# Stick-breaking sums from high and low parts in float32r, with one more stage in their pipeline

## The chip, the core and the metric

The kernel runs on one core of a Trainium2 chip. The metric is the device time of one execution in microseconds (us); three executions of the kernel before gave 1900.29, 1902.61 and 1904.76 us, and the median, 1902.61 us, is the time that the prediction is compared with. TensorE (PE) does the matrix products, VectorE (DVE), ScalarE (ACT) and GpSimd (POOL) the elementwise work, and SyncE (SP) issues the transfers. Each engine works through its own queue in order.

## The reference, cut to what matters

Two layers of a decoder trunk act on a sequence of 256 tokens with 1024 channels. A layer projects its input once, runs four mixers on the result (block-sparse attention, retention, a state-space mixer called SSD, and stick-breaking attention), projects and merges them, and then applies a feed-forward part: dense in the first layer, two of eight experts in the second. The change is in the stick-breaking attention, of 8 heads of width 64:

```python
z = jnp.einsum('bqhd,bkhd->bhqk', qb, k).astype(jnp.float32) * scale
causal = kpos[None, :] < qpos[:, None]
log_beta = jax.nn.log_sigmoid(z)
log_1mb = jnp.where(causal, jax.nn.log_sigmoid(-z), 0.0)
rem = lax.cumsum(log_1mb, axis=3, reverse=True) - log_1mb
w = jnp.where(causal, jnp.exp(log_beta + rem), 0.0).astype(v.dtype)
return jnp.einsum('bhqk,bkhd->bqhd', w, v)
```

For each query the logarithms `log_1mb` are summed over all later keys (the reversed cumulative sum), and the exponentials of score plus sum are the weights of the values. The kernel works with L = softplus(z) = -log_1mb, whose sum including the key itself is taken away from z. So the sums are products of L with a matrix of zeros and minus ones, and they are added in PSUM to the scores that already stand there.

## The kernel before, in words

**The stream of weights.** All weights come from HBM as tiles of 128x2048 numbers (`raw`, 1 MB each). SP issues one transfer for each tile, in an order fixed when the program is built. A tile is used in two halves of 128x1024. For each half ACT copies it to float32r (`whi`, L310), and DVE subtracts that copy from the original (`wlo`, L317). PE then forms each product as three float32r matmuls, high by high, high by low and low by high (`mm3`, L417 to L419). A half is 24 such matmuls of 256 columns, or 12 of 512. Five halves can be held in split form, and `half` (L351) lets the split run up to three halves ahead of the one that PE multiplies (AHEAD = 3).

**The side work.** After the matmuls of each half, `half` calls `step()` once, at some places twice, and one step of a list of tasks is written into the program there. The tasks are generators: the mixers (`ssd_task`, `sb_task`, `moba_task`, `ret_task`), and a few smaller ones. The schedule is manual: an instruction stands in its engine's queue where the code issued it. So what stands between two parts of a task is the work of the halves: on ACT the copies `whi` and the evacuations of finished PSUM banks (L724, L710 and others), on DVE the subtractions `wlo` and the weighted sums of adaLN tiles (L473, two for each tile), on PE the 24 or 12 matmuls.

**Stick-breaking.** `sb_task` (L924) handles the 8 heads as four pairs, with the helper `pipeline` (L745): each pair goes through seven stages, a new pair begins every third step, and within a step the later stages are issued first. The stages before are: `scores` (PE, into two PSUM banks), `soft` (two DVE operations for each head at L949 and L950, then an exponential and a logarithm on ACT at L953 and L954), `plus` (POOL: an addition at L958, and `strict`, L932, which zeroes the entries that are not strictly causal), `sums` (PE, three float32 matmuls for each head, L963 to L965), `weights` (for each head DVE clips the diagonal blocks at L971, ACT takes the exponential at L973, POOL applies `strict`), `out_` (`values`, PE, L739 and L742), and `end` (`split` of the result into float32r parts: ACT L426 and DVE L427). With a step of three, one step issues `end`, `sums` and `scores` of three successive pairs, the next `weights` and `soft`, the third `out_` and `plus`. The pool `px` gives this side work four PSUM banks of 512 numbers in each partition (two pairs' scores), and `w3` gives six tiles of 128x384.

The constant NT (128x128, zeros and minus ones) and NEGO (a column of minus ones, read 128 times) are slices of the tile `cst`, in float32.

## Time and profile before

| | us |
|---|---|
| median of three executions | 1902.61 |
| the profiled execution's own time | 1908.61 |
| its span, first to last instruction | 1906.6 |
| PE busy | 1862.5 (98%) |
| DVE busy | 1592.1 (84%) |
| ACT busy | 1194.6 (63%) |
| POOL busy | 186.6 (10%) |

The profiled execution took 6.0 us more than the median, and 2.0 us of it lie outside its span. The mean granted TensorE clock was 0.992 of full speed. A row of a timeline gives the start in us from the start of the span, the busy time, the engine and the line of the code; "xN" says that N instructions of one kind stand in one row. Matmuls overlap in their pipeline, so their cost is read from the distance between the starts of two rows, not from the busy time. A number in brackets at the end of a row is the time that the engine sat idle just before it, with what released it.

### The profile page before, as it was taken

To read this page: it belongs to the slowest core of one execution; us is meant where nothing else is said; L and a number is where in the kernel's file an instruction comes from. 1 tells how busy PE (TensorE), PEld (TensorE's weight loads), DVE (VectorE), ACT (ScalarE), POOL (GpSimd) and SP (SyncE) were. 2 spreads that over 40 slices of the span, in tenths; PEclk is the share of its full clock that TensorE was granted. 3 is DMA by queue.
4 is the path that set the end of the run, shared out by engine and by line. 5 is a ranking of instruction groups with operands and counts; after the bars stand their busy time and mean duration, and the time that the engine had idled before them with its cause. 6 is when DMAs were issued, how large, how long until landed. Compare 5 with 4: busy or idle time off the path is not lost.

```text
span 1906.6 us, 28966 instructions
## 1 busy us (share of the span) xinstructions
PE 1862.5 (98%) x11162; PEld 1627.6 (85%) x11162; DVE 1592.1 (84%) x2009; ACT 1194.6 (63%) x1507; POOL 186.6 (10%) x205
## 2 busy tenths in 40 slices
PE   6999999999999999999999999999999999999997
PEld 5888999899989889999888888888888888888885
DVE  7777877787766787768899989989899899999997
ACT  4545634454446356444677777777777777777774
POOL 0023332000000123320000000000000000000000
PEclk9999999999999999999899999999999999999999
DMA  9565666587745465656899999999999999999992
GB/s 354 185 242 210 228 234 220 185 282 285 286 168 208 164 250 201 243 177 242 330 383 331 350 369 372 393 373 352 366 375 388 379 343 376 355 403 375 388 401 110
DMA packets 86804, 565.99 MB, mean 297 GB/s; under 512 B 10241, under 2 KB 10497, under 8 KB 24706
## 3 DMA queue, kind: packets, MB, share of 16 engines
q1 hardware_dynamic: 82226, 550.30, 76.7%
q0 software_dynamic: 4288, 13.65, 2.2%
q8 instruction: 89, 1.46, 0.3%
q14 instruction: 57, 0.47, 0.1%
q10 hardware_dynamic: 144, 0.11, 0.0%
HBM read 557.21 MB, written 6.82 MB: 296 GB/s over the span
## 4 chain that ended last, share of the span: by engine, by line
PE 92%; DVE 3%; DMA 2%; issue 1%; ACT 1%; POOL 0%; SPq 0%; DVEq 0%; ACTq 0%; POOLq 0%
PE mm L417 23%; PE mm L419 22%; PE mm L418 22%; PE mx L419 6%; PE mx L418 6%; PE mx L417 6%; PE mx L1540 1%; DMA raw<-in_win_dram 1%; PE mx L1407 1%; DMA raw<-in_adaT_dram 1%; PE mx L739 1%; DVE wlo L317 1%; DVE raw L473 0%; PE mx L963 0%; DVE a L781 0%
## 5 line engine op out<-in xcount | busy, mean ns | idle before, releaser
L317 DVE TENSOR_TENSOR wlo<-raw,whi 128x1024 fp32r<-128x1024 f32 (+1 forms) x878 | 1036.4, 1223 | 188.8 <-ACT whi L310 187.1
L310 ACT ACTIVATE whi<-raw 128x1024 fp32r<-128x1024 f32 (+1 forms) x880 | 879.6, 1050 | 127.2 <-DMA raw<-in_win_dram 23.8
L417 PE MATMUL mm<-whi,ghi 128*128 128x512 f32 x896 | 350.3, 391 | 0.0
L419 PE MATMUL mm<-whi,glo 128*128 128x512 f32 x896 | 349.1, 390 | 0.0
L418 PE MATMUL mm<-wlo,ghi 128*128 128x512 f32 x896 | 348.7, 389 | 0.0
L417 PE MATMUL mm<-hhi,whi 128*128 128x256 f32 x1024 | 293.1, 286 | 14.0 <-ACT whi L310 14.0
L419 PE MATMUL mm<-hhi,wlo 128*128 128x256 f32 x1024 | 286.4, 280 | 0.9 <-DVE wlo L317 0.9
L418 PE MATMUL mm<-hlo,whi 128*128 128x256 f32 x1024 | 286.3, 280 | 0.0
L417 PEld LDWEIGHTS mm<-hhi,whi 128*128 128x128 f32 x1024 | 194.4, 190 | 22.6 <-ACT whi L310 16.4
L419 PEld LDWEIGHTS mm<-whi,glo 128*128 128x128 f32 x896 | 168.2, 188 | 35.8
L418 PEld LDWEIGHTS mm<-wlo,ghi 128*128 128x128 f32 x896 | 168.2, 188 | 34.9 <-DVE wlo L317 0.2
L417 PEld LDWEIGHTS mm<-whi,ghi 128*128 128x128 f32 x896 | 168.2, 188 | 34.2
L419 PEld LDWEIGHTS mm<-hhi,wlo 128*128 128x128 f32 x1024 | 194.5, 190 | 1.4 <-DVE wlo L317 1.4
L418 PEld LDWEIGHTS mm<-hlo,whi 128*128 128x128 f32 x1024 | 194.5, 190 | 0.7 <-issue 0.5
L417 PE MATMUL mx<-whi,ehi 128*128 128x512 f32 x448 | 179.6, 401 | 0.0
L419 PE MATMUL mx<-whi,elo 128*128 128x512 f32 x448 | 175.1, 391 | 0.0
L418 PE MATMUL mx<-wlo,ehi 128*128 128x512 f32 x448 | 174.9, 390 | 0.0
L426 ACT ACTIVATE ehi<-mx 128x512 fp32r<-128x512 f32 x56 | 33.6, 600 | 112.9 <-PE mx L1540 112.9
L419 PEld LDWEIGHTS mx<-whi,elo 128*128 128x128 f32 x448 | 84.1, 188 | 18.0
L418 PEld LDWEIGHTS mx<-wlo,ehi 128*128 128x128 f32 x448 | 84.3, 188 | 16.4 <-DVE wlo L317 0.8
L417 PEld LDWEIGHTS mx<-whi,ehi 128*128 128x128 f32 x448 | 84.2, 188 | 15.7
L1500 POOL DMA_INDIRECT outs<-lnt,row x14 | 14.4, 1026 | 807.0 <-DVE lnt L1494 804.8
(382 smaller groups left out, 2921.5 us busy)
## 6 DMA issues: line engine op xcount, KB each, us to landing
raw<-in_egu_dram SPq DMA_DIRECT2D x205, 1024.0 KB, 7.4
raw<-in_edn_dram SPq DMA_DIRECT2D x96, 1024.0 KB, 7.3
raw<-in_win_dram SPq DMA_DIRECT2D x79, 1024.0 KB, 4.9
raw<-in_adaT_dram SPq DMA_DIRECT2D x31, 1024.0 KB, 5.4
raw<-in_fgu_dram SPq DMA_DIRECT2D x22, 1024.0 KB, 5.6
raw<-in_adaR_dram SPq DMA_DIRECT2D x16, 1024.0 KB, 4.9
raw<-in_wbr_dram SPq DMA_DIRECT2D x16, 1024.0 KB, 4.9
raw<-in_fdn_dram SPq DMA_DIRECT2D x11, 1024.0 KB, 5.0
```

The lines of the kernel that those rows point to most:

```text
L310: act.activation(hi[:, c], raw, AF.Copy)
L317: dve.tensor_sub(lo[:, c], raw, hi[:, c].bitcast(F32))
L417: pe.matmul(ps, a[0], b[0], start=start, stop=False, **kw)
L418: pe.matmul(ps, a[0], b[1], start=False, stop=False, **kw)
L419: pe.matmul(ps, a[1], b[0], start=False, stop=stop, **kw)
L426: act.activation(hi, src, AF.Copy)
L739: pe.matmul(o[64 * j:64 * j + 64, :], v[:, 0, 128 * p + 64 * j:128 * p + 64 * j + 64], ws[j][:, 0:256], start=True, stop=False, skip_group ...
L1407: pe.matmul(o, xs[t][part][:, k * P:(k + 1) * P], dsp[:, t].rearrange("p a b -> p (a b)"), start=(n == 0), stop=(n == 3))
L1500: nc.gpsimd.indirect_dma_start(outs[c][:, :], bass.IndirectOffsetOnAxis(ap=row[:, 0:1], axis=0), y, None)
L1540: pe.transpose(pt[:, k * P:(k + 1) * P], g[:, k * P:(k + 1) * P], ident)
```

## The change

The tile L of each head is split like a weight, into a float32r copy on ACT and the remainder on DVE, in a new stage `parts_` between `plus` and `sums`; each head takes two more tiles of `w3` for it. `sums` multiplies both parts with NT and NEGO, which are now float32r: six matmuls of one pass for each head in place of three float32 matmuls, each of which the trace shows as two instructions. The number of stages stays at seven, because the former `end` (the split of the result) now stands in the same stage as `values`. The constants move into a tile of their own, `negs`, filled once by a transfer from POOL and a copy on ACT in the SSD task of the first layer.

```diff
--- before.py
+++ after.py
@@ -42,8 +42,8 @@
     _i += 2 * _c
 NWIN = _i
 
-C_ID, C_M3, C_NT, C_AL, C_IO, C_NEG, C_DEC, C_END = np.cumsum(
-    [0, 128, 384, 128, 384, 257, 1, 1536]).tolist()
+C_ID, C_M3, C_AL, C_IO, C_NEG, C_NT, C_DEC, C_END = np.cumsum(
+    [0, 128, 384, 384, 257, 1, 128, 1536]).tolist()
 S_C, S_CW, S_CB, S_DS, S_NG, S_GG, S_GB, S_L1G, S_L1B, S_L2G, S_L2B, S_DTB, S_AL, S_SDT, S_BA, S_END = np.cumsum(
     [0, 8, 32, 8, 4, 4, 4, 4, 8, 8, 8, 8, 8, 8, 64, 48]).tolist()
 
@@ -433,7 +433,9 @@
     crow = rowp.tile([P, D], F32, name="crow", bufs=1)
     nc.sync.dma_start(crow[0:1, :], I["c"])
     nc.scalar.dma_start(sm[0], I["sm"][0])
-    cst = cp.tile([P, C_DEC], F32, name="cst")
+    cst = cp.tile([P, C_NEG], F32, name="cst")
+
+    negs = cp.tile([P, 129], F32R, name="negs")
     rt = cp.tile([P, 72], F32, name="rt")
     x = [xp.tile([P, D], F32, name=f"x{t}") for t in range(2)]
     xT = I["xT"].rearrange("p k t -> p (k t)")
@@ -446,8 +448,7 @@
     mask3 = cst[:, C_M3:C_M3 + 384]
     U = cst[:, C_M3:C_M3 + 128]
     ONE = one.to_broadcast([P, P])
-    NT = cst[:, C_NT:C_NT + 128]
-    NEGO = cst[:, C_NEG:C_NEG + 1].to_broadcast([P, P])
+    NEGO, NT = negs[:, 0:1].to_broadcast([P, P]), negs[:, 1:129]
     ALI = cst[:, C_AL:C_AL + 384]
     iota = cst[:, C_IO:C_IO + 257]
 
@@ -677,8 +678,8 @@
         def a4(dt=F32):
             return mp.tile([P, 1024], dt, name="a4", bufs=9)
 
-        def w3():
-            return mp.tile([P, 384], F32, name="w3", bufs=6)
+        def w3(dt=F32):
+            return mp.tile([P, 384], dt, name="w3", bufs=6)
 
         def part_T(pss, kh, k1, rhs, evac=None):
 
@@ -790,6 +791,9 @@
             yield from need("xbc")
             xs_, bcm = T["xca"]
             two = mp.tile([40, 256], F32R, name="two", bufs=1)
+            if l == 0:
+                raw = w3()[:, 0:129]
+                nc.gpsimd.dma_start(raw, I["cst"][:, C_NEG:C_DEC])
             act.activation(pick, ident[0:40, 0:8], AF.Copy)
             act.activation(pick[32:40], ident[32:40, 32:40], AF.Copy)
             pool.memset(two.bitcast(F32), 0.0)
@@ -815,6 +819,8 @@
             act.activation(ee, ee, AF.Exp)
             ea = mp.tile([P, 8], F32, name="ea", bufs=1)
             act.activation(ea, s[:, S_AL:S_AL + 8], AF.Exp)
+            if l == 0:
+                act.activation(negs, raw, AF.Copy)
             yield
 
             cbt = []
@@ -958,11 +964,18 @@
                     pool.tensor_tensor(L, L, m, op=ALU.add)
                     strict(L)
 
+            def parts_(p):
+                for j, (m, L) in enumerate(LL[p]):
+                    LL[p][j] = hi, lo = w3(F32R), w3(F32R)
+                    split(hi, lo, L)
+
             def sums(p):
-                for z, (m, L) in zip(zz[p], LL.pop(p)):
-                    pe.matmul(z[:, 0:256], NT, L[:, 0:256], start=False, stop=True, skip_group_check=True)
-                    pe.matmul(z[:, 128:256], NEGO, L[:, 256:384], start=False, stop=True, skip_group_check=True)
-                    pe.matmul(z[:, 256:384], NT, L[:, 256:384], start=False, stop=True, skip_group_check=True)
+                for z, hl in zip(zz[p], LL.pop(p)):
+                    for L in hl:
+                        pe.matmul(z[:, 0:256], NT, L[:, 0:256], start=False, stop=True, skip_group_check=True)
+                        pe.matmul(z[:, 256:384], NT, L[:, 256:384], start=False, stop=True, skip_group_check=True)
+                    for L in hl:
+                        pe.matmul(z[:, 128:256], NEGO, L[:, 256:384], start=False, stop=True, skip_group_check=True)
 
             def weights(p):
                 ww[p] = []
@@ -976,12 +989,10 @@
 
             def out_(p):
                 values(zz[p][0][:, 0:256], p, bv, ww.pop(p))
-
-            def end(p):
                 split(o[0][:, p], o[1][:, p], zz.pop(p)[0][:, 0:256])
                 if p == 3:
                     ready.add(("o", 3))
-            yield from pipeline((scores, soft, plus, sums, weights, out_, end), 4, 3)
+            yield from pipeline((scores, soft, plus, parts_, sums, weights, out_), 4, 3)
 
 
         def moba_task():
@@ -1681,7 +1692,7 @@
     build_order()
     aside[2] = [(x[0], xT[:, 0:D])]
     aside[5] = [(x[1], xT[:, D:2 * D])]
-    aside[14] = [(cst, I["cst"][:, 0:C_DEC])]
+    aside[14] = [(cst, I["cst"][:, 0:C_NEG])]
     aside[24] = [(sm[1], I["sm"][1]), (rt, I["rt"])] + [(x[t], I["x"][t * P:(t + 1) * P, :]) for t in range(2)]
     emit_dma(RAW)
     hT = hT0 = new_hT()
```

A step now issues `out_` with the result's split, `parts_` and `scores` together, the next `sums` and `soft`, the third `weights` and `plus`. The instructions move so:

On VectorE, layer 0, from the split of one pair's output to the next pair's clip. `wlo` is a half's low part, `raw,mod` an adaLN sum, `mx` a PSUM bank of scores, `olo` the result's low part. Before, the clip (L971) stands ahead of the next pair's `soft` (L949, L950):

```order
L427 TENSOR_TENSOR olo<-mx,ohi 128x256
L473 SCALAR_TENSOR_TENSOR raw,mod_1595<-raw,crow 128x1024 x2
L317 TENSOR_TENSOR wlo<-raw,whi 128x1024
L971 TENSOR_SCALAR mx<-mx 128x2x128 x2
L949 TENSOR_SCALAR w_1624<-mx 128x384
L950 SCALAR_TENSOR_TENSOR w_1625<-w_1624,mx 128x384
L949 TENSOR_SCALAR w_1628<-mx 128x384
L950 SCALAR_TENSOR_TENSOR w_1629<-w_1628,mx 128x384
L725 COPY a_1497<-mm 128x512
L317 TENSOR_TENSOR wlo<-raw,whi 128x1024 x2
L427 TENSOR_TENSOR olo<-mx,ohi 128x256
```

After, with L984 for the clip and L955, L956 for `soft`:

```order
L427 TENSOR_TENSOR olo<-mx,ohi 128x256
L427 TENSOR_TENSOR w_1602<-w_1538,w_1601 128x384
L427 TENSOR_TENSOR w_1606<-w_1542,w_1605 128x384
L474 SCALAR_TENSOR_TENSOR raw,mod_1615<-raw,crow 128x1024 x2
L317 TENSOR_TENSOR wlo<-raw,whi 128x1024
L955 TENSOR_SCALAR w_1648<-mx 128x384
L956 SCALAR_TENSOR_TENSOR w_1649<-w_1648,mx 128x384
L955 TENSOR_SCALAR w_1652<-mx 128x384
L956 SCALAR_TENSOR_TENSOR w_1653<-w_1652,mx 128x384
L726 COPY a_1503<-mm 128x512
L317 TENSOR_TENSOR wlo<-raw,whi 128x1024
L984 TENSOR_SCALAR mx<-mx 128x2x128 x2
```

The two subtractions of `parts_` (L427 on `w`) are new, and the clip of a pair now stands behind the next pair's `soft` and one more `wlo`.

On ScalarE, the same place. `ohi` is the result's high part, `whi` a half's, `w` a tile of `w3`; before, the exponentials of the weights (L973) come ahead of `soft`'s (L953, L954):

```order
L426 ACTIVATE ohi<-mx 128x256
L310 ACTIVATE whi<-raw 128x1024
L973 ACTIVATE w_1617<-mx 128x384
L973 ACTIVATE w_1621<-mx 128x384
L953 ACTIVATE w_1625<-w_1625 128x384
L954 ACTIVATE w_1625<-w_1625 128x384
L953 ACTIVATE w_1629<-w_1629 128x384
L954 ACTIVATE w_1629<-w_1629 128x384
L724 ACTIVATE a_1497<-mm 128x512
L310 ACTIVATE whi<-raw 128x1024 x2
```

After, with L986 for the weights and L959, L960 for `soft`:

```order
L426 ACTIVATE ohi<-mx 128x256
L426 ACTIVATE w_1601<-w_1538 128x384
L426 ACTIVATE w_1605<-w_1542 128x384
L310 ACTIVATE whi<-raw 128x1024
L959 ACTIVATE w_1649<-w_1649 128x384
L960 ACTIVATE w_1649<-w_1649 128x384
L959 ACTIVATE w_1653<-w_1653 128x384
L960 ACTIVATE w_1653<-w_1653 128x384
L725 ACTIVATE a_1503<-mm 128x512
L310 ACTIVATE whi<-raw 128x1024
L986 ACTIVATE w_1696<-mx 128x384
L986 ACTIVATE w_1700<-mx 128x384
```

The weights' exponentials went behind the four operations of `soft`, an evacuation and a `whi`, and two copies of `parts_` stand behind `ohi`.

On TensorE, layer 0, from the third pair's values (L739, L742) to the fourth pair's sums (L963 to L965), with a half of 24 matmuls between them before (`...` leaves out the other matmuls of that half):

```order
L739 MATMUL mx<-w_1752,a_789 64x256
L739 MATMUL mx<-w_1756,a_789 64x256
L742 MATMUL mx<-w_1752,a_789 64x128
L742 MATMUL mx<-w_1756,a_789 64x128
L417 MATMUL mm<-hhi,whi 128x256
...
L419 MATMUL mm<-hhi,wlo 128x256
L963 MATMUL mx<-w_1760,cst 128x256
L964 MATMUL mx<-w_1760,cst 128x128
L965 MATMUL mx<-w_1760,cst 128x128
L963 MATMUL mx<-w_1764,cst 128x256
```

After, with L740 and L743 for the values and L975 to L978 for the sums:

```order
L740 MATMUL mx<-w_1843,a_792 64x256
L740 MATMUL mx<-w_1847,a_792 64x256
L743 MATMUL mx<-w_1843,a_792 64x128
L743 MATMUL mx<-w_1847,a_792 64x128
L975 MATMUL mx<-w_1894,negs 128x256
L976 MATMUL mx<-w_1894,negs 128x128
L975 MATMUL mx<-w_1895,negs 128x256
L976 MATMUL mx<-w_1895,negs 128x128
L978 MATMUL mx<-w_1894,negs 128x128
L978 MATMUL mx<-w_1895,negs 128x128
L975 MATMUL mx<-w_1898,negs 128x256
```

The half that stood between values and sums is gone from there: the fourth pair's sums follow the third pair's values at once. It is the only place of its kind; elsewhere at least one half of the stream still stands between these stages.

## Rows read from the trace of the kernel before

**Rows 1.** Page, parts 1 and 4: PE's busy time, and the chain's shares by engine.

```profile
PE 1862.5 (98%) x11162; PEld 1627.6 (85%) x11162; DVE 1592.1 (84%) x2009; ACT 1194.6 (63%) x1507; POOL 186.6 (10%) x205
...
PE 92%; DVE 3%; DMA 2%; issue 1%; ACT 1%; POOL 0%; SPq 0%; DVEq 0%; ACTq 0%; POOLq 0%
```

**Rows 2.** Windows: us, busy (xcount) PE, PEld, DVE, ACT, POOL; PEclk, DMA, GB/s.

```profile
133.00:187.00 54.00, 54.00 (x404) 48.51 (x403) 39.78 (x55) 30.30 (x47) 19.90 (x24) 1.00 0.54 197
676.00:730.00 54.00, 54.00 (x404) 48.52 (x403) 38.91 (x60) 33.04 (x50) 17.82 (x24) 1.00 0.61 221
```

**Rows 3.** Timeline of PE, layer 0: start us, us, engine line op tiles xcount.

```profile
142.20 0.28 PE L419 MATMUL mm<-hhi,wlo 128*128 128x256 f32 x1
142.32 0.60 PE L963 MATMUL mx<-w,cst 128*128 128x256 f32 x2
142.75 0.38 PE L964 MATMUL mx<-w,cst 128*128 128x128 f32 x2
...
143.20 0.60 PE L963 MATMUL mx<-w,cst 128*128 128x256 f32 x2
...
144.17 0.70 PE L939 MATMUL mx<-a,a 64*128 64x256 f32 x4
...
145.02 0.50 PE L417 MATMUL mm<-whi,hhi 128*128 128x512 f32 x1
```

**Rows 4.** Timeline of PE, third pair's scores done, second pair's values start.

```profile
157.09 0.50 PE L417 MATMUL mm<-whi,hhi 128*128 128x512 f32 x1
...
162.87 0.44 PE L739 MATMUL mx<-w,a 128*64 128x256 f32 x2
```

**Rows 5.** Timeline of PE, last pair's values and the next half.

```profile
183.20 0.65 PE L739 MATMUL mx<-w,a 128*64 128x256 f32 x4
...
184.00 0.38 PE L417 MATMUL mm<-hhi,whi 128*128 128x256 f32 x1
```

**Rows 6.** Timeline of VectorE, one turn of the pipeline.

```profile
153.98 1.21 DVE L473 SCALAR_TENSOR_TENSOR raw<-raw,crow 128x1024 f32<-128x1024 f32 x1
...
156.26 1.22 DVE L317 TENSOR_TENSOR wlo<-raw,whi 128x1024 fp32r<-128x1024 f32 x1
157.40 0.75 DVE L971 TENSOR_SCALAR mx<-mx 128x256 f32<-128x256 f32 x2
158.07 0.54 DVE L949 TENSOR_SCALAR w<-mx 128x384 f32<-128x384 f32 x1
...
159.84 0.56 DVE L950 SCALAR_TENSOR_TENSOR w<-w,mx 128x384 f32<-128x384 f32 x1
```

**Rows 7.** Timeline of ScalarE, the same turn and the next.

```profile
157.91 0.87 ACT L973 ACTIVATE w<-mx 128x384 f32<-128x384 f32 x2 [4.93 <-DVE mx L971]
...
161.42 0.58 ACT L724 ACTIVATE a<-mm 128x512 f32<-128x512 f32 x1
161.90 1.99 ACT L310 ACTIVATE whi<-raw 128x1024 fp32r<-128x1024 f32 x2
...
172.88 1.28 ACT L710 ACT_TABLE_LOAD   x1
```

**Rows 8.** Timeline of GpSimd, the same turn.

```profile
158.47 0.79 POOL L932 TENSOR_SCALAR_AFFINE_SELECT w<-w 128x256 f32<-128x256 f32 x2 [5.83 <-ACT w L973]
160.47 1.02 POOL L958 TENSOR_TENSOR w<-w,w 128x384 f32<-128x384 f32 x1 [1.20 <-ACT w L954]
161.56 0.41 POOL L932 TENSOR_SCALAR_AFFINE_SELECT w<-w 128x256 f32<-128x256 f32 x1
...
163.03 1.45 POOL L932 TENSOR_SCALAR_AFFINE_SELECT w<-w 128x256 f32<-128x256 f32 x1
```

**Rows 9.** Timeline of PE, one-column matmuls, each with its own weights.

```profile
304.81 1.28 PE L902 MATMUL mx<-one,a 128*128 128x1 f32 x11
```

**Rows 10.** Windows (columns as Rows 2) at two pauses of PE.

```profile
289.00:296.00 7.00, 5.73 (x22) 4.95 (x23) 4.06 (x5) 4.03 (x7) 0.00 (x0) 0.56 0.48 158
807.00:811.00 4.00, 1.89 (x17) 1.70 (x16) 1.76 (x3) 2.49 (x3) 0.00 (x0) 1.00 0.46 180
```

**Rows 11.** Timeline of PE, the ends of those two pauses [idle before <-releaser].

```profile
289.16 0.38 PE L417 MATMUL mm<-ohi,whi 128*128 128x256 f32 x1 [2.16 <-ACT ohi L426]
...
809.85 0.38 PE L1077 MATMUL mx<-a,w 128*128 128x128 f32 x1 [2.11 <-DVE w L1071]
```

## The prediction

> **What bounds the kernel now.** I read the page first: PE is busy for 1862.5 us, 98% of the span, and 92% of the chain that ended last is PE's [rows 1]. So time is lost where PE gains work or has to wait. Then the two stretches of stick-breaking, 54 us in each layer: PE is busy for all of both, at the full granted clock (1.00), DVE for 39.78 and 38.91 us and ACT for 30.30 and 33.04 [rows 2]. Nothing there ends later than PE, so the four side engines' work is free as long as each result comes before PE reaches the instruction that wants it. How much earlier it comes is the question, and the timelines answer it. The second pair's weights are ready when the second `strict` ends at 158.47 + 0.79 = 159.26 [rows 8]; PE reaches their values at 162.87 [rows 4]. That is a spare of 3.6 us, a little more than one half: two halves lie between 157.09 and 162.87 [rows 4], so a half is 2.89 us.
>
> **What PE saves.** A head's three float32 sums take 143.20 - 142.32 = 0.88 us: 0.43 for the 256 columns and (143.20 - 142.75) / 2 = 0.22 for each of 128 [rows 3]. After the change a head has two matmuls of 256 columns and four of 128 in float32r. The first cost 0.12 each (142.20 to 142.32) [rows 3]. For a float32r matmul of 128 columns there is no row. Half of the 256-column price is 0.06, the float32 price 0.22. The nearest row is one where the load of 128x128 weights, and not the columns, sets the pace: 11 one-column matmuls in 1.28 us, 0.116 each [rows 9]. I take 0.115, so a head takes 0.24 + 4 × 0.115 = 0.70, and 16 heads save 16 × 0.18 = 2.9 us (from +6.7 with 0.06 to a loss of 3.8 with 0.22).
>
> The Trainium skill ("TensorE: Matmul & The Clock Gate", section "Back-to-back issue gap") gives about 81 ns for each load-and-matmul pair of 128 columns. With it the saving would be 16 × 0.32 = 5.1 us; the row above says 0.116 for a narrow matmul, and it is the one that I keep.
>
> **What is added beside PE.** Sixteen copies on ACT and sixteen subtractions on DVE of 128x384. The nearest rows are the exponentials of that shape on ACT, 0.87 for two, say 0.5 each with the start, and DVE's 0.54 [rows 6, 7]: 8 and 9 us in all, on engines with at least 21 and 14 us to spare in each stretch [rows 2]. As work they cost nothing; as links of a chain they count, below. The constants' transfer and copy come once, early, in a task that nothing hurries: 0.
>
> **What moves: the chain between two pairs' weights.** Before, the clip of a pair stands on DVE ahead of the next pair's `soft`, and its chain from clip to weights takes 159.26 - 157.40 = 1.86 us [rows 6, 8]. After, the order is another. `plus` of pair p+1 waits on POOL behind `strict` of pair p; `parts_` of p+1 waits for `plus`, `soft` of p+2 stands behind `parts_` on DVE, and the clip of p+1 behind that `soft` and another `wlo`, whose `whi` stands on ACT behind `soft`'s logarithms and an evacuation. So from the weights of p to those of p+1 there is one serial chain. Its links:
> - `plus` and `strict` for two heads: from 160.47 to 163.03 + 1.45 is 4.0; with 0.41 as at 161.56 for both `strict` it is 2 × (1.02 + 0.41) = 2.9 [rows 8]. I take 3.4.
> - `parts_`: a copy 0.5, the last subtraction 0.55.
> - the adaLN sum 2.28 (153.98 to 156.26) and a `wlo` 1.14 (156.26 to 157.40) [rows 6].
> - `soft` on DVE: 159.84 + 0.56 - 158.07 = 2.33 [rows 6]; then the last head's exponential and logarithm, until the evacuation starts at 161.42 [rows 7]: 1.0.
> - the evacuation 0.48 and a `whi` 1.0 (161.42, 161.90, 1.99 for two) [rows 7], a `wlo` 1.14.
> - clip to weights 1.86.
>
> The sum is 15.7 us. In the same time PE itself has three halves (8.67), values 0.80 (183.20 to 184.00) [rows 5], scores 0.85 (144.17 to 145.02) [rows 3] and two heads' sums 1.40: 11.7. PE waits for the difference, before the values, in each turn, since the chain starts anew from the weights that were late.
>
> Turn by turn. In both layers the first pair's weights come 5.5 us later than their place before would give them (`soft` 2.33, 1.0, `whi` 1.0, `wlo` 1.14) against the spare of 3.6: 1.9 late. Layer 0:
> - first to second pair: 15.7 - 11.7 = 4.0.
> - second to third: no adaLN sum ahead of `soft`, but a `whi` (1.0) and `wlo`; the exponentials change tables around an evacuation, 1.28 each time [rows 7]. 3.4 + 0.5 + 1.0 + 1.14 + 2.33 + 1.0 + 1.28 + 0.48 + 1.0 + 1.14 + 1.28 + 1.86 = 16.4, less 11.7: 4.7.
> - third pair's values to the fourth's sums: no half lies between. `plus` 3.4 and `parts_` 1.05 against 0.80 of values: 3.6, and 0.3 more behind it before the last values.
>
> Layer 0 together 14.5. Layer 1 has other work in between:
> - first to second: no adaLN sum, and the same as above without tables: 13.9, less 11.7: 2.2.
> - second to third: no split between `soft` and the clip: 10.7, against two halves and 3.05: 1.9.
> - third to fourth: 4.45 against 0.80 and one half: 0.8.
>
> With the first 1.9 that is 6.8. Both layers: 21.3 us of waiting. The bounds: with `plus` at 2.9 or 4.0 each of the seven turns moves by 0.5 or 0.6, so by 3.5 to 4; the first pairs' spare may be a half larger or smaller, 2 to 5 us in both layers.
>
> **Sum.** The profiled execution took 1908.6 us; + 21.3 - 2.9 gives 1927.0. The median of the runs lies 6.0 below it, and I carry the difference over: 1902.6 + 18.4 = **1921 us**. What is late next after each wait is the same chain one pair on, which is why the waits add up. While PE waits, the split gets ahead by up to three halves, but that gives PE nothing back afterwards: it is busy throughout both stretches now, so it waits for no split there [rows 2].
>
> **Rivals.**
> - *The waits stay hidden.* If chain and PE run level (11.7 or less), only the saving is left: 1902.6 - 2.9 = 1899.7. For it: DVE and ACT are idle for a third of the stretch. Against: that idle time is just this kind of waiting, and 4 us would have to come off the chain, more than any one of its bounds gives. 0.12.
> - *The narrow float32r matmuls cost as the float32 ones* (0.22), so PE loses 3.8 where I let it save 2.9. For it: nothing but that no row shows one. It adds 6.7: 1927.7. Without the waits it would be slower than before by itself, from 0.16 for each narrow matmul. 0.05.
> - *PE's clock falls at the new waits.* After a pause of 2.16 us [rows 11] the window of 7 us from 289 to 296 has a mean granted clock of 0.56 [rows 10], near the lower level (1.2 of 2.4 GHz): some 3 us lost. After one of 2.11 us at 809.85 [rows 11] it stayed at 1.00 [rows 10]. Three new waits are longer than both (4.0, 4.7, 3.6): 3 × 3 = 9, so 1930. 0.13.
>
> The Trainium skill speaks for this last one: by "TensorE: Matmul & The Clock Gate", section "HAM oscillation — how this bites in real kernels", an engine that keeps stopping for its inputs is thrown back to the slow clock each time. The trace agrees at one of those two pauses and not at the other.
>
> - *The change doesn't do what it says*, that is, the sums remain in several passes: the code gives both operands as float32r, and such matmuls already run in one pass at 0.12 [rows 3]. Below 0.01, left out.
>
> **How the numbers follow.** My forecast has 0.70, with its own range of 1910 to 1929: the bounds of waits and narrow matmuls taken together rather than all at one end. What a measurement of this kernel can tell from no change is about 0.2%, 3.8 us: 1898.8 to 1906.4. The hidden case's 1899.7 lies just inside that band, and with 0.10 or less for a narrow matmul it lies below it, so its 0.12 is shared evenly between faster and same, 0.06 each. Of my forecast's 0.70, waits of which most are covered put 0.03 into faster and 0.04 into same. That gives 0.09 faster, 0.10 same and 0.81 slower. The range that holds 8 in 10 leaves out the hidden case and the far end of a falling clock: 1904 to 1933.
>
> **What the changed profile would show.** Right: a head's sums 0.70 us apart; in both stretches PE busy for less than the whole, by about 14 and 7 us; PE idle before L740 with POOL's `strict` (L938) as releaser, and once in layer 0 before L975, released by L427 or L426; DVE idle before L427 on the tiles of `w3`, waiting for POOL. Wrong: PE busy throughout both stretches, or waits that do not grow from the order of DVE and ACT but stand before scores or the stream's L417; a head's sums at 0.88 or more; a granted clock near 0.5 behind the waits would speak for the third rival.

## The result, and the profile after

The changed kernel takes 1934.1 us (median of four executions, 1932.0 to 1940.0), the kernel before 1903.7 in the runs taken with it: 1.0166 times as long, 95% interval 1.0151 to 1.0182, or 30.4 us more. I had forecast 1921, which was 18.4 more. The profiled execution took 1932.7 us, 24.0 more than that of before; the difference between 24.0 and 30.4 is a part of the miss and comes back below.

The page of the profile after, PE's busy time and the chain's shares (against [rows 1]):

```profile
PE 1870.1 (97%) x11162; PEld 1631.3 (84%) x11162; DVE 1600.0 (83%) x2025; ACT 1204.6 (62%) x1526; POOL 186.5 (10%) x206
...
PE 85%; DVE 6%; ACT 3%; DMA 2%; issue 2%; POOL 1%; SPq 0%; DVEq 0%; ACTq 0%; POOLq 0%
```

PE now has 85% of the chain in place of 92%; DVE, ACT and POOL have gained 3, 2 and 1 points. The losses lie where they were expected. Here are the two stretches of stick-breaking after the change, 80 us each: us, busy time of PE, weight loads, DVE, ACT, POOL, then the granted clock, the DMA share and GB/s:

```profile
130.00:210.00 80.00, 71.69 (x482) 62.55 (x481) 49.98 (x71) 45.20 (x68) 18.23 (x24) 0.89 0.47 167
686.00:766.00 80.00, 71.66 (x516) 62.96 (x516) 53.13 (x85) 44.60 (x73) 19.38 (x24) 0.96 0.48 174
```

PE was busy throughout at a granted clock of 1.00 before [rows 2]. Now it is idle for 8.3 us in each (the prediction had about 14 and 7), and the mean clock has fallen to 0.89 and 0.96; at a slow clock PE counts as busy. The waits, from PE's timeline (the bracket is the idle time just before the row, and what released it), first layer 0, then layer 1:

```profile
151.87 0.81 PE L740 MATMUL mx<-w,a 128*64 128x256 f32 x3 [0.55 <-POOL w L938]
...
154.64 0.79 PE L945 MATMUL mx<-a,a 64*128 64x256 f32 x1 [0.89 <-DVE olo L427]
...
171.43 0.48 PE L945 MATMUL mx<-a,a 64*128 64x256 f32 x1 [0.89 <-DVE olo L427]
...
185.85 1.49 PE L740 MATMUL mx<-w,a 128*64 128x256 f32 x4 [3.75 <-POOL w L938]
...
189.30 0.58 PE L975 MATMUL mx<-w,negs 128*128 128x256 f32 x1 [1.53 <-ACT w L426]
...
190.67 0.58 PE L975 MATMUL mx<-w,negs 128*128 128x256 f32 x1 [0.69 <-DVE w L427]
...
709.98 0.81 PE L740 MATMUL mx<-w,a 128*64 128x256 f32 x3 [2.97 <-POOL w L938]
...
726.39 0.65 PE L740 MATMUL mx<-w,a 128*64 128x256 f32 x2 [0.67 <-POOL w L938]
...
727.73 0.43 PE L740 MATMUL mx<-w,a 128*64 128x256 f32 x1 [0.69 <-POOL w L938]
...
738.88 0.81 PE L740 MATMUL mx<-w,a 128*64 128x256 f32 x3 [1.30 <-POOL w L938]
...
752.52 0.81 PE L740 MATMUL mx<-w,a 128*64 128x256 f32 x3 [1.94 <-POOL w L938]
```

L740 is a pair's values, waiting for POOL's `strict`; L975 in layer 0 is the fourth pair's sums, right behind the third pair's values, waiting for the parts: both as the prediction said. It had not said that L945, the scores, would wait, and had even named waits there as a sign against it: their second head goes into the PSUM bank that the result's split (`olo`) has just left.

The saving on PE stands in one head's sums of the same trace:

```profile
144.29 0.28 PE L975 MATMUL mx<-w,negs 128*128 128x256 f32 x1
144.41 0.22 PE L976 MATMUL mx<-w,negs 128*128 128x128 f32 x1
144.47 0.33 PE L975 MATMUL mx<-w,negs 128*128 128x256 f32 x1
144.64 0.22 PE L976 MATMUL mx<-w,negs 128*128 128x128 f32 x1
144.70 0.39 PE L978 MATMUL mx<-w,negs 128*128 128x128 f32 x2
144.93 0.33 PE L975 MATMUL mx<-w,negs 128*128 128x256 f32 x1
```

From 144.29 to 144.93 a head takes 0.64 us, against 0.88 [rows 3] and 0.70 in the forecast. With 0.12 for each of the two wide ones, a narrow one costs 0.10 on the mean; by the starts themselves the wide ones take 0.12 and 0.17, the two of L976 0.06 each, and the two of L978 0.115 each. The Trainium skill ("TensorE: Matmul & The Clock Gate", section "Back-to-back issue gap") has 81 ns for 128 columns, and an estimate by it makes the head 0.56; the measurement lies between that and the 0.70 from the row of one-column matmuls that I used [rows 9].

What the stretches come to is best seen as turns: the time from one pair's first value matmul to the next pair's, in us, read from the starts in the traces (L739, or L740 after the change). Under "forecast" are the turns that the prediction's sums give (for the third turn in layer 0: values 0.8, wait 3.6, sums 1.4, a half 2.9, wait 0.3; in layer 1: 10.9 and 0.8):

```
                               layer 0             layer 1
before                         12.1  12.0   8.3     9.4   9.3  11.0
forecast                       15.7  16.4   9.0    13.9  10.7  11.7
after                          16.8  17.2  11.2    16.4  12.5  13.6
order alone                    13.9  14.8   9.8    13.4  10.1  11.0
parts in the step of the sums  11.6  11.8   8.1    14.3   9.0  12.4
more tiles                     16.2  15.8  12.1    16.5  10.1  13.6
parts on POOL                  16.9  17.7  12.8    17.0  13.0  18.9
unread matmuls                 16.3  17.4  11.3    14.5  12.5  13.6
no strict on the logarithms    15.4  16.3  12.1    16.5  11.2  12.6
tiles and unread matmuls       16.2  17.9   9.9    14.2  14.0  12.1
the same, no strict            15.2  16.0  10.4    13.1  11.1  12.7
```

Each row is one execution. The turns hold the same halves of the stream before and after, but for two: the third of layer 0 has one half in place of two, the first of layer 1 three in place of two, so these two compare only through the sum; the row of the parts in the step of the sums holds the halves of before, the other rows those of the changed kernel. The six turns took 62.2 us before and 87.7 after; the forecast had 77.4.

The whole stretches are measured between the same matmuls of the stream in both traces. Layer 0 goes from 130.12 to 200.04 us before and from 128.29 to 213.88 after, 15.7 us longer; layer 1 from 675.11 to 755.02 and from 686.26 to 779.15, 13.0 longer; together 28.7. The forecast, waits less saving, was 13.0 and 5.4. With the measured saving on the sums added back, 1.9 us in each layer, waits and slow clock took 17.6 and 14.9 us, 32.5 in all, where the prediction had 21.3.

The chain of the first turn of layer 0 is the one that was predicted. POOL first (`strict` of the first pair's weights, then `plus` and `strict` of the second pair):

```profile
151.41 0.79 POOL L938 TENSOR_SCALAR_AFFINE_SELECT w<-w 128x256 f32<-128x256 f32 x2 [12.71 <-ACT w L986]
152.17 1.00 POOL L964 TENSOR_TENSOR w<-w,w 128x384 f32<-128x384 f32 x1
153.24 1.28 POOL L938 TENSOR_SCALAR_AFFINE_SELECT w<-w 128x256 f32<-128x256 f32 x1
154.49 0.99 POOL L964 TENSOR_TENSOR w<-w,w 128x384 f32<-128x384 f32 x1
155.55 0.61 POOL L938 TENSOR_SCALAR_AFFINE_SELECT w<-w 128x256 f32<-128x256 f32 x1
```

Then ACT's copies of the parts, behind POOL:

```profile
154.55 0.52 ACT L426 ACTIVATE w<-w 128x384 fp32r<-128x384 f32 x1 [1.01 <-POOL w L938]
156.19 0.52 ACT L426 ACTIVATE w<-w 128x384 fp32r<-128x384 f32 x1 [1.12 <-POOL w L938]
```

Then DVE, from the last part to the clip (L984), with `soft` (L955, L956) between:

```profile
156.75 0.56 DVE L427 TENSOR_TENSOR w<-w,w 128x384 fp32r<-128x384 f32 x1 [0.85 <-ACT w L426]
157.23 1.22 DVE L474 SCALAR_TENSOR_TENSOR raw<-raw,crow 128x1024 f32<-128x1024 f32 x1
...
159.51 1.22 DVE L317 TENSOR_TENSOR wlo<-raw,whi 128x1024 fp32r<-128x1024 f32 x1
160.65 0.55 DVE L955 TENSOR_SCALAR w<-mx 128x384 f32<-128x384 f32 x1
...
162.19 0.56 DVE L955 TENSOR_SCALAR w<-mx 128x384 f32<-128x384 f32 x1 [0.40 <-PE mx L978]
...
165.99 1.23 DVE L317 TENSOR_TENSOR wlo<-raw,whi 128x1024 fp32r<-128x1024 f32 x1 [1.98 <-ACT whi L310]
167.14 0.75 DVE L984 TENSOR_SCALAR mx<-mx 128x256 f32<-128x256 f32 x2
```

From the weights at 152.17 to the next at 169.0 it runs: POOL to 156.16, copy and subtraction to 157.31, adaLN sum and `wlo` to 160.7, `soft` to 163.4, logarithm, evacuation, `whi` and `wlo` to 167.1, clip to weights. Two things are longer than in the sum: POOL's part is 4.0 and not 3.4, and the second head's maximum waits for L978, the previous pair's sums, because the six tiles of `w3` are used up and the tile it gets is one that those sums read.

### The profile page after: what moved, and what is told of

It is laid out like the page before. It is cut to its first block, busy times and chain, and to the rows that moved or that the text cites. A ratio compares the mean times of both kernels' runs of the same rounds, so it can differ in the third digit from the quotient of the medians.

```text
span 1930.6 us, 28966 instructions
## 1 busy us (share of the span) xinstructions
PE 1870.1 (97%) x11162; PEld 1631.3 (84%) x11162; DVE 1600.0 (83%) x2025; ACT 1204.6 (62%) x1526; POOL 186.5 (10%) x206
## 4 chain that ended last, share of the span: by engine, by line
PE 85%; DVE 6%; ACT 3%; DMA 2%; issue 2%; POOL 1%; SPq 0%; DVEq 0%; ACTq 0%; POOLq 0%
PE mm L417 21%; PE mm L418 20%; PE mm L419 20%; PE mx L418 6%; PE mx L419 6%; PE mx L417 6%; DVE wlo L317 2%; PE mx L1551 1%; PE mx L1418 1%; ACT whi L310 1%; DMA raw<-in_adaT_dram 1%; DVE raw L474 1%; DMA raw<-in_win_dram 1%; PE mx L740 1%; DMA lnt<-in_lnp_dram 0%
## 5 line engine op out<-in xcount | busy, mean ns | idle before, releaser
L417 PEld LDWEIGHTS mm<-hhi,whi 128*128 128x128 f32 x1024 | 194.8, 190 | 21.2 <-ACT whi L310 15.7
L1511 POOL DMA_INDIRECT outs<-lnt,row x14 | 14.3, 1025 | 805.9 <-DVE lnt L1505 803.8
```

The costliest lines, as they stand in the source:

```text
L417: pe.matmul(ps, a[0], b[0], start=start, stop=False, **kw)
L1511: nc.gpsimd.indirect_dma_start(outs[c][:, :], bass.IndirectOffsetOnAxis(ap=row[:, 0:1], axis=0), y, None)
```

## The experiments

All times are medians beside runs of the kernel before on the same chip, whose median was 1903.9 to 1905.4. Ratios are to before, with 95% intervals.

**Order alone, parts alone.** First, the changed order with the sums left in float32:

```diff
-            def end(p):
                 split(o[0][:, p], o[1][:, p], zz.pop(p)[0][:, 0:256])
-            yield from pipeline((scores, soft, plus, sums, weights, out_, end), 4, 3)
+            yield from pipeline((scores, soft, plus, None, sums, weights, out_), 4, 3)
```

> The stages stand in the changed kernel's order (the result's split merged into the stage of the values, an empty stage where the parts were), but the sums stay in float32 and no parts are made. Order theory (the clip and the exponentials of a pair's weights stand behind the next pair's soft, so the chain from weights to weights is longer than PE's own turn): most of the loss stays. Against the changed kernel's 1934 it loses the parts' link, 1.05 us in each of six turns (-6), and gives up PE's saving (+3.8, from 0.64 us for a head's sums in place of 0.88): about 1931, 1922 to 1937. Work theory (the loss comes from the added copies and subtractions on ScalarE and VectorE): back to before, 1904 within 4.

1918.0 us, ratio 1.0056 (1.0038 to 1.0073): about 11 us of loss, a third of the change's. Neither theory had this. Without parts no DVE instruction waits for POOL: in the trace `plus` ends at 159.24 and `soft` starts at 161.39, behind DVE's own work and without a wait. So POOL's link falls out of the chain together with the parts', and the chain is shorter by more than the link that I took off.

Then the parts, in the order of before:

```diff
             def sums(p):
+                parts_(p)
...
-            yield from pipeline((scores, soft, plus, parts_, sums, weights, out_), 4, 3)
+            yield from pipeline((scores, soft, plus, sums, weights, out_, end), 4, 3)
```

> The sums are made of high and low parts as in the changed kernel, but the stages stand as before: the parts are made in the step of the sums, just ahead of them, and the result's split has its own stage again. Order theory: the weights stand ahead of soft again, so only PE's saving is left, 16 times 0.24 = 3.8 us: 1900, 1896 to 1907. Work theory: the same copies and subtractions are there, so 1925 to 1935.

1914.0 us, ratio 1.0047 (1.0031 to 1.0064): slower by 9 where the order theory had faster by 4. The parts are late for the sums by themselves, and after the pause the clock falls. PE's first sums in layer 0, and the 10 us around them:

```profile
143.60 0.38 PE L976 MATMUL mx<-w,negs 128*128 128x256 f32 x1 [1.93 <-DVE w L427]
```

```profile
140.00:150.00 10.00, 8.07 (x46) 6.73 (x45) 8.47 (x13) 5.38 (x11) 2.00 (x4) 0.83 0.87 315
```

So order and parts cost 11 and 9 us apart, which adds up to 20, and 31.6 by the ratio when both are there. Links of one chain would do that; but the parts stand at another place in the two kernels, so it is no clean test of it.

**More tiles.** The maxima of `soft` and the weights go into tiles that other tasks have left:

```diff
-                    m, L = w3(), w3()
+                    m, L = mp.tile([P, 2, 260], F32, name="pad", bufs=2).rearrange("p a b -> p (a b)")[:, 0:384], w3()
...
-                w = w3()
+                w = mp.tile([P, 384], F32, name="cbt", bufs=2)
```

> The changed kernel with two more tiles for the maxima in soft and two more for the weights, taken from tiles that other tasks have finished with, so that the six tiles of 128x384 hold only the logarithms and their parts, and soft no longer waits for the sums of the pair before it. Tile theory (the growth beyond the predicted waits, some 12 us, comes from those waits for tiles): 1920 to 1925. Order theory: the trace shows 2.0 and 0.4 us of such waits, so at most 4 us come back: 1930 to 1934.

1929.9, ratio 1.0117 (1.0093 to 1.0142): 4 us below the changed kernel by the medians and 9 by the ratios, so between the order theory (at most 4) and the tile theory (9 or more); the tiles are a part, and the smaller one.

> The parts in the step of the sums, stages as before, and the four further tiles as well. Order theory: PE does not wait in either, so the same as without the further tiles, 1900 within 3. Tile theory: faster than without them by more than 3.

1911.7, ratio 1.0040 (1.0024 to 1.0055): within 3 of the run without the tiles, but both at 1912 to 1914 and not at 1900.

**Parts on POOL.**

```diff
-                    split(hi, lo, L)
+                    pool.tensor_copy(hi, L)
+                    pool.tensor_tensor(lo, L, hi.bitcast(F32), op=ALU.subtract)
```

> The changed kernel's order of stages, with both operations of the parts (the float32r copy and the subtraction) on GpSimd behind strict, so that no instruction on VectorE or ScalarE waits for GpSimd's plus in front of the next pair's soft. Queue theory (the loss needs both the order and the parts, because the parts wait for plus at the head of VectorE's and ScalarE's queues and hold up soft and the clip behind them): as with the order alone, less PE's saving of 3.8: 1914, 1908 to 1920. Length theory (only the sum of the links from weights to weights counts): GpSimd's four operations are some 3.6 us in place of 1.05, so 2.5 us more in each of six turns: 1949, and not under 1934.

1945.8, ratio 1.0223 (1.0196 to 1.0249). The length theory has it, in the sum: a longer link on POOL costs another 11 to 12 us, even though nothing on DVE or ACT waits for `plus` in front of `soft` any more. It does not come as 2.5 us in each turn, though: of the 8.6 us by which the turns grew, 5.3 are in the last turn of layer 1 and 0.1 to 0.6 in each of the first two of both layers.

**Weights in the step of the sums.**

```diff
+            def sums_weights(p):
+                sums(p)
+                weights(p)
...
-            yield from pipeline((scores, soft, plus, parts_, sums, weights, out_), 4, 3)
+            yield from pipeline((scores, soft, plus, parts_, sums_weights, out_, end), 4, 3)
```

> The parts are a stage of their own, as in the changed kernel, but the weights are issued in the same step as the sums, right behind them and ahead of the next pair's soft, and the result's split has its own stage as before. Order theory: no half of the stream and no soft stands between sums and clip, one half stands between parts and sums, and clip to weights (1.86 us) fits into the half ahead of the values: only PE's saving is left, 1905.4 - 3.8 = 1902, 1898 to 1906. Rival: VectorE now waits at the clip for PE in each turn and loses its lead, so the time is as with the parts in the step of the sums, 1910 to 1915.

> The same with the four further tiles. Order theory: 1902, within 3 of the kernel without them. Tile theory: faster than without them by more than 3.

1925.0 and, with the four tiles, 1922.3, ratios 1.0112 (1.0085 to 1.0140) and 1.0098 (1.0071 to 1.0124). The rival's mechanism was right, and its price (1910 to 1915) too low. DVE waits at the clip until PE has made the sums (3.5 and 4.1 us in the first two turns of layer 1), everything behind comes late, and PE stands at the scores until the old result's split has left the bank (L945, layer 1):

```profile
722.21 0.48 PE L945 MATMUL mx<-a,a 64*128 64x256 f32 x1 [3.18 <-DVE olo L427]
```

**Is it the clock?** Three stretches behind waits of PE, after the change (columns as for the windows above; the clock is the third number from the end):

```profile
153.00:160.00 7.00, 6.11 (x19) 4.48 (x18) 5.62 (x9) 2.38 (x4) 3.01 (x4) 0.62 0.41 150
190.00:198.00 8.00, 7.33 (x43) 6.89 (x44) 3.08 (x6) 3.68 (x6) 0.87 (x3) 0.65 0.36 132
711.00:718.00 7.00, 7.00 (x21) 4.97 (x19) 4.02 (x6) 3.04 (x6) 2.25 (x4) 0.51 0.25 105
```

These means lie between the two levels, 1.2 and 2.4 GHz, and near the lower one in layer 1. By the Trainium skill ("TensorE: Matmul & The Clock Gate", section "HAM oscillation — how this bites in real kernels") an engine that keeps stopping for its inputs falls back each time; the trace agrees at three places, and not behind the waits of 1.30 and 1.94 us in layer 1, where the clock stayed at 1.00. Length times one minus the clock, summed over the windows of both stretches in which it was below 1.00, comes to some 12 us. To see what they cost, matmuls that nobody reads were put into PE's waits:

```diff
+                for _ in range({(0, 1): 24, (0, 2): 24, (1, 0): 24, (1, 1): 12, (1, 2): 12}.get((l, p), 0)):
+                    pe.matmul(full[p + 1][:, 384:512], negs[:, 1:129], negs[:, 1:129], start=False, stop=True, skip_group_check=True)
                 values(zz[p][0][:, 0:256], p, bv, ww.pop(p))
```

> The changed kernel with float32r matmuls of 128 columns that nobody reads, in unused columns of a score bank, ahead of five of the eight values: 24 (2.8 us) before the second and third pair's in layer 0 and the first pair's in layer 1, 12 before the second and third pair's in layer 1, so that PE is not idle where it waited. Clock theory (much of the loss is the slow clock after the waits; the two layers' stretches show 10.8 us of it): up to 8 us faster than the changed kernel, 1926 to 1930. Chain theory (the chain of the side engines sets the pace, and what PE loses to its clock it would have waited anyway): 1934 within 4.

1933.3, ratio 1.0153 (1.0129 to 1.0178): within the range of the chain theory. The clock was back at 1.00 behind the first waits of both layers, where by that sum it had cost 3.4 us each; those two turns fell by 0.5 and 1.9 us, and the values still waited for POOL in the first. So more than half of what PE loses to its clock there it would have waited. The rest is not tested: from 186 to 198 us the mean clock was still 0.57, and it fell anew behind the last wait of layer 1 (0.76 from 753 to 760). Nor can four runs of this spread tell a gain of 2 or 3 us from none.

In the last turn of layer 0 the slow clock does cost time by itself. After the change, the half ahead of the last pair's values, POOL's `strict` on their weights, and the values:

```profile
192.86 0.52 PE L417 MATMUL mm<-hhi,whi 128*128 128x256 f32 x1
195.12 0.79 POOL L938 TENSOR_SCALAR_AFFINE_SELECT w<-w 128x256 f32<-128x256 f32 x2 [5.04 <-ACT w L986]
197.04 0.65 PE L740 MATMUL mx<-w,a 128*64 128x256 f32 x4
```

The weights are ready at 195.91, and PE comes to them 1.1 us later without a wait, because the half took 4.18 us and not 2.89 [rows 4]. The kernels with the parts in the step of the sums show the same: the first turn of layer 1 took 14.3 us at a mean clock of 0.76, and 11.2 at 1.00 in the profiled execution of the one with more tiles, though the tiles differ as well.

**A shorter link.**

```diff
                     pool.tensor_tensor(L, L, m, op=ALU.add)
-                    strict(L)
```

> The changed kernel without strict on the logarithms (their entries that are not strictly causal are left in). Chain theory: GpSimd's link, plus and strict for two heads, falls from the 3.9 us that the changed kernel's trace shows to 2.0, and PE waits that much less in each of six turns: 1934 - 11 = 1923, 1918 to 1928. Rival (the loss comes from waits for tiles, banks or the clock, and GpSimd's link is covered): 1934 within 4.

1933.5, ratio 1.0166 (1.0145 to 1.0186): no gain in the median, against my theory. The four runs reach from 1925.7 to 1935.3, and the trace is that of the fastest: its turns are 3.6 us shorter than those of the changed kernel, not 11. One reason is POOL: without `strict` between them the two additions take 2.9 us in three of the six turns (1.95 in the others), so the link there fell by 1.05 to 1.4 us and not by 1.9. Another is in the first turn of layer 1, where `soft` then waited all the longer for the tile that PE's sums release, first after the change, then in this run:

```profile
719.25 0.56 DVE L955 TENSOR_SCALAR w<-mx 128x384 f32<-128x384 f32 x1 [2.04 <-PE mx L978]
```

```profile
715.24 0.56 DVE L955 TENSOR_SCALAR w<-mx 128x384 f32<-128x384 f32 x1 [2.97 <-PE mx L977]
```

**Several limits at once.** The next theory was that in a turn there stand, close behind each other, the chain of the side engines, PE at the slow clock, and `soft`'s wait for a tile through PE. Two and then three remedies were taken together: the four tiles, the unread matmuls (12 and 24 before the second and third pair's values in layer 0, 24 before the first pair's in layer 1), and `strict` on the logarithms, each by the edit shown above.

> The changed kernel with the four further tiles and with unread float32r matmuls ahead of three values: 12 and 24 before the second and third pair's in layer 0, 24 before the first pair's in layer 1. Theory of several limits (in a turn the chain of the side engines, PE behind the slow clock, and soft's wait for a tile that PE's sums release lie within some 2 us of each other, so that taking one away shows the next): both together gain more than each alone, 5 to 9 us below the changed kernel, 1925 to 1929. Theory of one chain (the side engines' links alone set every turn): no more than each alone, 1930 to 1934.

> The same, and strict on the logarithms left out, so that GpSimd's link is shorter (2.9 us in place of 4.0 in the trace without strict, since its second addition then takes twice as long). Theory of several limits: the shorter link now shows in five or six turns, about 1 us each: 1920 to 1924. Theory of one chain, by the run without strict alone: 1930 to 1934.

1930.8, ratio 1.0136 (1.0099 to 1.0173), and 1922.6, ratio 1.0094 (1.0069 to 1.0120). The first is inconclusive: its runs reach from 1924 to 1934, and in its trace the clock fell all the same (0.81 and 0.65 in the second and third turn of layer 0, 0.76 in the second of layer 1), so the slow clock was not taken away. The second is clear of noise, 1921.5 to 1924.4 against 1932.0 to 1940.0: the three together bring 11.5 us.

Whether that is more than their sum is not settled. By the medians each alone brought 4.2, 0.8 and 0.6. By the ratios it is 9.3, 2.5 and 0.0, against 13.7 together, and in the table's turns 3.4, 2.1 and 3.6, against 9.3: there they simply add up. So the runs do not show that one limit hides behind another.

**The rest.** The merged split by itself:

```diff
-            yield from pipeline((scores, soft, plus, sums, weights, out_, end), 4, 3)
+            yield from pipeline((scores, soft, plus, sums, weights, out_), 4, 3)
```

> The kernel before, with only the split of the result moved into the stage of the values, one step earlier. Order theory: the split is early there and nothing waits for it: 1905 within 3. Rival (the split's copy, which waits for PE's values, now stands at the head of ScalarE's queue and holds up the copies of the weights' halves): 1910 or more.

1902.8, ratio 1.0001 (0.9987 to 1.0014): it costs nothing.

The parts in the stage of `plus`, with the four tiles:

```diff
                     strict(L)
+                for j, (m, L) in enumerate(LL[p]):
+                    LL[p][j] = hi, lo = w3(F32R), w3(F32R)
+                    split(hi, lo, L)
```

> Stages as before, the four further tiles, and the parts made in the step of plus, right behind it, so a half of the stream lies between parts and sums. Chain theory by the links alone (clip, soft, plus, parts, and the splits between: about 12 us, PE's turn 11.7): PE finds the parts ready, 1902 to 1907. Queue theory (VectorE's subtraction now waits for GpSimd's plus in front of two wlo and the next clip): slower than with the parts in the step of the sums (1912), 1915 to 1925.

1911.7, ratio 1.0056 (1.0035 to 1.0077): between the two theories, and no better than in the step of the sums.

The high part alone:

```diff
-                    LL[p][j] = hi, lo = w3(F32R), w3(F32R)
-                    split(hi, lo, L)
+                    hi, = LL[p][j] = (w3(F32R),)
+                    act.activation(hi, L, AF.Copy)
```

> Stages as before, with the float32r copy alone: the low parts and their matmuls are left out. PE has three narrow-priced matmuls for a head, 0.32 us in place of 0.88: 9 us saved if it shows in full, 1896, 1893 to 1900 (the saving is real and the subtraction on VectorE is what eats it). Rival (the copy behind plus is late for the sums by itself, as the parts in the step of the sums were, by some 12 us in all): 1905 to 1910.

1903.3, ratio 1.0005 (0.9991 to 1.0019). PE has some 9 us less to do by the prices above, and nothing of it can be measured. In the trace layer 0 is 3.2 us shorter than in that of the merged split; in layer 1 the three turns took 31.3 us against 29.7, with 2.7 us of waits for the copy at the sums.

No version here beats the kernel before.

## Why the prediction missed

The direction, the mechanism and most of the places were right: PE waits at the values for POOL, and at the fourth pair's sums for the parts, because the clip stands behind the next pair's `soft`. The order alone lost 11 us, the merged split nothing, and a longer link on POOL 11 to 12 more. Layer 0 was sized fairly, 13.0 us against 15.7. The time lies 1.1 us above my range, and the miss, 30.4 - 18.4 = 12.0, has three parts.

- *The waits were too short*: 28.7 measured against 18.4, so 10.3, of which 7.6 in layer 1. The failed step is "Both layers: 21.3 us of waiting", and in it layer 1's share: 6.8 there, where waits and slow clock took 14.9 (and 17.6 in place of 14.5 in layer 0). Each turn's sum lacks 0.8 to 2.5 us. POOL's link was 3.9 to 4.3 in five of the six turns, and I took 3.4 (bounds 2.9 to 4.0, and for seven turns where six have this link). The first pairs' waits, 1.9 each in the sum, were 0.55 and 2.97. In layer 1's first turn PE ran at a clock of 0.51 behind its first wait, so its sums came late, and `soft` waited 2.0 us for their tile; I had counted tiles as free. At the end of that turn the adaLN sums ran beside the two `strict`, which took 2.41 us and not 0.79 [rows 8]. In layer 1's third turn I all but stopped at the sums, though behind them stand another adaLN sum and a clip. In layer 0's third turn the sums and the half behind them ran mostly at the slow clock, which my sum did not have.
- *The offset*: I carried over that the profiled execution of before lay 6.0 above the median of three. It lay 4.9 above the median of four, and the profiled execution after lies 1.5 below its own. Adding the difference of profiles to the median loses these 6.4 us.
- The rest of the trace gives back 4.7, mainly 1.8 ahead of layer 0 and 2.7 from 280 to 300 us of the trace before, where its clock had fallen [rows 10].

The forecast had neither of the last two parts, and that they nearly cancel is luck.

The saving was mis-sized the other way, 3.8 and not 2.9 (and at 0.06 for a narrow matmul it would have been 6.4, not the 6.7 of the prediction). The third rival, the falling clock, occurred at three places, though only the fall at 185 us belongs to a wait that it named. As a sum "waits plus clock" it would have counted much of the same time twice, since more than half of the slow time at two of the places was hidden in waits. But it is not nothing: by the turns 0.5 and 1.9 us there, and at least 1.1 at the third. Not settled is which limit ends each single turn, and whether one hides another.

## What to carry to other kernels

Before a stage is added to a software pipeline, follow the chain from one iteration's last step to the next one's through all queues, buffers included, and compare it with the bound engine's own turn: work of 0.5 us on an idle engine cost here because the turn had only 3.6 us of spare. Where several limits may lie close together, taking one away can show little, so lengthen a link as well (or take away several) to see whether it counts, and take enough runs to tell the sum of the single gains from the joint one. A saving on the bound engine is not a gain before the engines that feed it are shown to keep up: some 9 us less of matmuls moved nothing that could be measured.

## What the runs showed of the hardware

POOL and DVE slow each other. In the changed kernel's layer 1 POOL's two `strict` took 2.41 us while DVE ran its adaLN sums (724.85 to 727.41, the second of them 1.42 in place of 1.21), and an addition took 1.96 while DVE ran a `wlo` (727.34 to 728.75, 1.41 in place of 1.22); a little later, without them, an addition took 1.01 and a `strict` 0.41:

```profile
725.26 2.41 POOL L938 TENSOR_SCALAR_AFFINE_SELECT w<-w 128x256 f32<-128x256 f32 x2 [11.87 <-ACT w L986]
727.64 1.96 POOL L964 TENSOR_TENSOR w<-w,w 128x384 f32<-128x384 f32 x1
729.67 0.41 POOL L938 TENSOR_SCALAR_AFFINE_SELECT w<-w 128x256 f32<-128x256 f32 x1
730.05 1.01 POOL L964 TENSOR_TENSOR w<-w,w 128x384 f32<-128x384 f32 x1
```

The Trainium skill ("SBUF — State Buffer", section "SBUF: two separate sides") has a rule for it: POOL and a DVE operation with two inputs from SBUF share a pair of ports, which the one that starts first keeps for its whole instruction while the other stands still. The adaLN sums and `wlo` are such operations, and the trace agrees: the addition ends 0.85 us after that `wlo`, and takes 1.96 against 1.01. So POOL's link, 3.1 to 4.3 us here, depends on what DVE runs beside it, which I had bounded [rows 8] without asking what sets it.

The same stretch of matmuls runs at two paces at the same granted clock. In 20 us of the dense feed-forward, PE started 173 matmuls in the profiled execution of before and 179 in that of the merged split, both at 1.00. Between the same matmuls, at 395 and 495 us before, that is 3.7 us; what sets the pace no run here shows:

```profile
450.00:470.00 20.00, 20.00 (x173) 20.00 (x172) 14.52 (x23) 8.71 (x14) 0.00 (x0) 1.00 0.75 279
```

```profile
450.00:470.00 20.00, 20.00 (x179) 20.00 (x178) 15.38 (x24) 9.28 (x15) 0.00 (x0) 1.00 0.80 287
```

And whether a pause brings the clock down is not fixed by its length alone. Ahead of the last values of layer 1 PE waited for 1.94 us in the changed kernel (752.52, above) and for 1.95 in the run with unread matmuls:

```profile
752.64 1.07 PE L740 MATMUL mx<-w,a 128*64 128x256 f32 x3 [1.95 <-POOL w L938]
```

In the 7 us that follow, the first kept 1.00 and the second had a mean of 0.76:

```profile
753.00:760.00 7.00, 7.00 (x61) 6.26 (x61) 4.27 (x5) 5.44 (x8) 0.00 (x0) 1.00 0.45 164
```

```profile
753.00:760.00 7.00, 7.00 (x47) 5.96 (x46) 2.93 (x4) 5.29 (x8) 0.00 (x0) 0.76 0.47 167
```
